# A decoder layer on one core: the opening stage computes its modulation sums, its normalised rows and its angles another way

## The chip, the cores and the metric

The kernel runs on one core of a Trainium2 chip. A core has five engines that run their own instruction streams: TensorE (PE in the profile, with PEld for its weight loads), VectorE (DVE), ScalarE (ACT), GpSimd (POOL) and SyncE (SP, which here only issues transfers). The metric is the device time of one execution in microseconds (us); lower is better.

## The reference, cut to what matters

The layer maps x (1024 rows of 1024 channels, float32) to an output of the same shape. A vector c gives six modulation vectors; the first two, shift sh1 and scale sc1, are used in the opening:

```python
cond = silu(c)
mod = einsum('bd,de->be', cond, w_ada) + b_ada     # 1024 x 6144 weights
sh1, sc1, gt1, sh2, sc2, gt2 = split(mod, 6)
h = rmsnorm(x, g_mix) * (1 + sc1) + sh1
proj = h @ w_in                                    # q, k, v, indexer q, indexer k, weights, conv
```

Then q, k and the indexer's q and k are rotated by angles `position * inv_freq`, top-k sparse attention and a causal convolution run side by side, `w_out` joins them, and an MLP of width 4096 and a final norm follow. Every product that the kernel takes for h is made of three products of two-part operands (a rounded part "hi" and the remainder "lo").

## The kernel before, in words

Everything is one Python function, `layer`, which writes instructions for all engines; a planner then lays out, ahead of the run, the order of each engine's instructions, by the number in `tc.cur_priority` and by its own estimate of when operands are ready. Each engine then runs its list strictly in that order. In the opening the number simply follows the order in which the lines are written; afterwards the table `PR` gives it by kind of work. Waits between engines are made from the data that instructions read and write, and a tile with `bufs=n` makes the next writer wait until the oldest of n copies is no longer read.

The opening stage lies in the pool `start`. Its loads are issued on SP in the order of the string `START`: x0 to x7 are the eight 128-row blocks of x (`xs`, 512 KB each), a0 to a3 are quarters of the first two modulation vectors' weights (`wa`, each quarter two tiles of 1 MB, one for contraction blocks 0 to 3, one for 4 to 7; four tiles in all, so that quarter 2 takes the space of quarter 0 and quarter 3 that of quarter 1), p0 to p2 are the pieces of `w_in` for k, v, the indexer's k and weights. Its work is written in the order of `WORK`:

- `row_scale(g)` takes the mean square of four blocks of rows, two by ACT (`Square`, L290) and two by DVE (L287), and makes for each block a diagonal matrix `dg` of 1/rms (L296); it is called for blocks 0 to 3 first and as step r4 for blocks 4 to 7.
- step t (`transposes`) multiplies the eight 128 x 128 parts of a block by `dg` on TensorE, which transposes and scales them (L309); ACT copies the result to `xT` (L310). t0 to t3 are the first half of the rows, t4 to t7 the second.
- step a (`ada`) sums, on DVE, a quarter's eight weight blocks times `cond` into `acc` (L318, seven times L316). Step e (`ada_end`) sums `acc` over partitions by four one-column matmuls into `pa` (L324) and finishes scale and shift in `modT` (L326 to L329). A quarter serves two of the eight channel blocks.
- step h (`h_cols`) makes two channel blocks of h for the first half of the rows: DVE scales in place in `xT` (L334), ACT writes the hi part (L335), DVE (channel blocks 0 to 5) or POOL (6 and 7) the lo part (L336). For the second half of the rows the same runs after all steps, with POOL for every lo part.
- step k (`kv`) adds two channel blocks to the k/v products of blocks 0 to 3 (L347), in four PSUM tiles (`mm`, `mc`).

After the steps the angles are computed from `positions` (L374 to L412): eight small products, a range reduction of some twenty dependent small DVE instructions, and three ACT instructions. When the pool is closed, the k/v products of blocks 0 to 3 are evacuated (L447 to L450: ACT and DVE), and the same four PSUM tiles take blocks 4 to 7 ("the second k/v round", again L347, 96 matmuls). Then come the projections for the indexer's q (L137), keys are rotated and stacked (L457 to L482), and the other four modulation vectors are summed on DVE from 512 KB loads (`ada_part`, loads L517, sums L521 and L523; `ada_row` L530, `ada_col` L537).

Of the kernel before, what the change touches and what calls it, by code (L numbers as in the profile page):

```python
# [9 lines left out]
FT = mybir.dt.float32  # L10
# [17 lines left out]
EPS = 1e-6  # L28
# [44 lines left out]
def layer(ctx, tc, x, c, positions, w_ada, b_ada, g_mix, w_in, conv_w, conv_b,  # L73
          conv_norm_g, conv_norm_b, w_out, g_mlp, w_up, w_down, g_final, out, dump=None):
    nc = tc.nc
    V, A, P, T, SP = nc.vector, nc.scalar, nc.gpsimd, nc.tensor, nc.sync
    x, positions = x[0], positions[0]
# [10 lines left out]
    def dbg(name, ap):  # L88
        if dump and name in dump:
            SP.dma_start(dump[name], ap)  # L90
# [134 lines left out]
    pieces = []  # L225
# [6 lines left out]
    def hblk(b, k, s):  # L232
        return hT[b // 4][s][:, k, (b % 4) * 128:(b % 4 + 1) * 128]
# [4 lines left out]
    hT = {}  # L238
    with tc.tile_pool(name="start", bufs=1, reuse_waits="tile") as st:
# [39 lines left out]
        ms, rs, tmp1 = (st.tile([128, 8], FT, name=n) for n in ("ms", "rs", "tmp1"))  # L279
        junk = st.tile([128, D], U8, name="junk")  # L280
        dg = {}

        def row_scale(g0):
            for b in range(g0, g0 + 4):
# [6 lines left out]
            col = slice(g0, g0 + 4)  # L291
            V.tensor_scalar(ms[:, col], ms[:, col], 1.0 / D, EPS, op0=OP.mult, op1=OP.add)
            rsqrt(rs[:, col], ms[:, col], tmp1[:, col], 4)
            for b in range(g0, g0 + 4):
                dg[b] = st.tile([128, 128], FT, name="dg", bufs=4)
                V.tensor_scalar(dg[b], ident, rs[:, b:b + 1], None, op0=OP.mult)  # L296

        for hf in range(2):  # L300
            hT[hf] = (half_tile("AC"[hf]), half_tile("BD"[hf]))
        pa = psum.tile([128, 16], FT, name="po")

        def transposes(b):
            for q in range(2):
                t = tp_tile()
                for j in range(4):
                    k = 4 * q + j
                    T.matmul(t[:, j, :], xs[b][:, k * 128:(k + 1) * 128], dg[b], start=True, stop=True)  # L309
                A.copy(xT[:, 4 * q:4 * q + 4, b * 128:(b + 1) * 128], t)  # L310

        def ada(jj):
# [6 lines left out]
            return acc  # L319

        def ada_end(jj, acc):
            for i in range(4):
                c0 = 8 * (i // 2) + 2 * jj + i % 2
                T.matmul(pa[:, c0:c0 + 1], acc[:, i * 128:(i + 1) * 128], ones[:, 0:1], start=True, stop=True)  # L324
            s0, s1 = slice(2 * jj, 2 * jj + 2), slice(8 + 2 * jj, 10 + 2 * jj)
            V.tensor_tensor(modT[:, s0], pa[:, s0], bada[:, s0], op=OP.add)  # L326
            a1 = modT[:, s1]
            V.tensor_tensor(a1, pa[:, s1], bada[:, s1], op=OP.add)
            V.scalar_tensor_tensor(a1, a1, 1.0, gmix[:, s0], op0=OP.add, op1=OP.mult)  # L329

        def h_cols(k, hf):
            hi, lo = hT[hf]
            xk = xT[:, k, hf * 512:(hf + 1) * 512]
            V.tensor_scalar(xk, xk, modT[:, 8 + k:9 + k], modT[:, k:k + 1], op0=OP.mult, op1=OP.add)  # L334
# [3 lines left out]
        kvps = {}  # L338

        def kv(k, blocks):  # L340
            for i, b in enumerate(blocks):
                if k == 0:
                    kvps[b] = (mm_tile if i < 2 else mc_tile)(328)
                hi, lo = hblk(b, k, 0), hblk(b, k, 1)
                wh, wl = pieces[k]
                for j, (l, r) in enumerate(((hi, wh), (lo, wh), (hi, wl))):
                    T.matmul(kvps[b], l, r, start=k == 0 and j == 0, stop=k == KD - 1 and j == 2)  # L347

        row_scale(0)
        accs = {}  # L350
        for step in WORK.split():
            n = int(step[1:])
            if step[0] == "a":
                accs[n] = ada(n)
            elif step[0] == "t":
                transposes(n)
            elif step[0] == "r":
                row_scale(n)
            elif step[0] == "e":
                ada_end(n, accs[n])  # L360
            elif step[0] == "h":
                for k in (2 * n, 2 * n + 1):
                    h_cols(k, 0)
            elif step[0] == "k":
                for k in (2 * n, 2 * n + 1):
                    kv(k, KVG[0])
            elif step[0] == "g":
                for k in (2 * n, 2 * n + 1):
                    h_cols(k, 1)
        for k in range(KD):  # L370
            if k // 2 not in [int(x[1:]) for x in WORK.split() if x[0] == "g"]:
                h_cols(k, 1)
        posf = st.tile([8, 128], FT, name="posf")
        V.tensor_copy(posf, posi)  # L374
        tq = tp_tile()
# [35 lines left out]
        V.tensor_scalar(ml, ml, -1.0, 1.5707963267948966, op0=OP.mult, op1=OP.add)  # L411
        A.activation(cs, ml, AF.Sin)  # L412

        tw = tp_tile()
# [4 lines left out]
        for k in range(KD):  # L419
            dbg("hT", xT[:, k, :]) if k == 0 else None  # L420
# [844 lines left out]
```

## Time and profile before

| | us |
|---|---|
| median of 3 runs | 1375.25 (1374.19 to 1385.54) |
| the profiled execution, whole | 1377.54 |
| its span, first to last instruction | 1375.8 |
| mean granted TensorE clock | 0.964 of full |
| PE busy | 1268.3 |
| DVE busy | 974.8 |
| ACT busy | 683.5 |
| POOL busy | 482.0 |

Times in the rows are microseconds from the span's start. A chain of waits names, step by step, what the last instruction was waiting for; a table of stretches gives each engine's busy time and the clock within it; a wait row names the instruction that waited, the one that released it, the total, the number of times and the longest.

### The profile page before, as it was taken

The page shows a single profiled execution, that of the slowest core. Times are in us where ns is not written, and L with a number is a line of the kernel's source. Part 1 is how long each engine was busy: PE and PEld are TensorE (multiplying, and loading weights), DVE is VectorE, ACT ScalarE, POOL GpSimd, SP SyncE. Part 2 cuts the span into 40 slices and gives each one's busy share as a digit, 9 for nine tenths or more (in the row PEclk, how much of TensorE's full clock was granted, in tenths as well). Part 3 has the DMA queues.
Part 4 walks back from the last instruction along what each step waited for, and adds up shares of the span by engine and source line. Part 5 has one row for each costly group of instructions (what it writes and reads, how often), then busy time and mean ns, then how long its engine had stood idle before and what let it go on. Part 6 is the DMA issues. An engine that isn't in the chain of part 4 may idle for free.

```text
span 1375.8 us, 19421 instructions
## 1 busy us (share of the span) xinstructions
PE 1268.3 (92%) x6686; PEld 1065.7 (77%) x6686; DVE 974.8 (71%) x2074; ACT 683.5 (50%) x1376; POOL 482.0 (35%) x396
## 2 busy tenths in 40 slices
PE   4677899989998899989999999899999999999997
PEld 4676789978887678767887879777878877888875
DVE  4879889999898899997878762473443386343457
ACT  3323358855764888768983552333122223333332
POOL 1333434422144234452223216422222244444453
PEclk9688999999999899999999999999999999999999
DMA  9337735522143123222111122352111134323332
GB/s 319 121 115 224 226 79 155 139 62 70 31 139 110 60 70 93 92 70 61 62 47 54 62 77 85 130 192 83 47 45 49 54 107 162 93 91 101 94 98 91
DMA packets 135690, 139.55 MB, mean 101 GB/s; under 512 B 8877, under 2 KB 109833, under 8 KB 135592
## 3 DMA queue, kind: packets, MB, share of 16 engines
q1 hardware_dynamic: 135424, 138.22, 32.2%
q8 instruction: 52, 0.85, 0.3%
q14 instruction: 46, 0.38, 0.1%
q10 hardware_dynamic: 168, 0.11, 0.0%
HBM read 126.23 MB, written 12.06 MB: 101 GB/s over the span
## 4 chain that ended last, share of the span: by engine, by line
PE 68%; DVE 21%; DMA 4%; issue 3%; ACT 3%; POOL 1%; ACTq 0%; POOLq 0%; DVEq 0%; SPq 0%
PE mm L126 25%; PE mc L126 13%; PE mm L137 9%; PE tp L126 7%; DMA wa<-in_w_ada_dram 3%; PE po L841 2%; PE tp L834 2%; DVE acc L521 2%; DVE cv L643 1%; PE tp L309 1%; PE po L748 1%; PE mc L592 1%; DVE acc L1018 1%; PE mc L822 1%; DVE acc L316 1%
## 5 line engine op out<-in xcount | busy, mean ns | idle before, releaser
L185 POOL TENSOR_TENSOR wlo<-wraw,whi 128x512 fp32r<-128x512 f32 x310 | 416.7, 1352 | 754.2 <-ACT whi L184 698.0
L184 ACT ACTIVATE whi<-wraw 128x512 fp32r<-128x512 f32 x310 | 193.9, 629 | 292.1 <-PE mm L126 143.1
L126 PE MATMUL mm<-half,whi 128*128 128x512 f32 x608 | 207.4, 407 | 0.6 <-ACT half L957 0.6
L680 ACT ACTIVATE sj<-score,bits 128x512 uint8<-128x512 f32 (+5 forms) x186 | 163.2, 877 | 23.0 <-DVE bits L683 11.0
L643 DVE SCALAR_TENSOR_TENSOR cv<-glu,cwT,cv 128x512 f32<-128x512 f32 x232 | 174.0, 750 | 0.8
L126 PE MATMUL mm<-whi,uh 128*128 128x512 f32 x344 | 141.7, 412 | 14.3 <-DVE sq L979 8.2
L126 PE MATMUL mc<-half,whi 128*128 128x512 f32 x416 | 149.0, 390 | 0.1
L126 PE MATMUL mm<-whi,ul 128*128 128x512 f32 x344 | 138.8, 404 | 3.0 <-DVE ul L986 3.0
L126 PE MATMUL mm<-wlo,uh 128*128 128x512 f32 x344 | 139.4, 405 | 0.0
L984 DVE TENSOR_TENSOR sq<-sq 128x512 f32<-128x512 f32 x42 | 46.0, 1096 | 126.1 <-ACT sq L983 126.1
L1018 DVE TENSOR_TENSOR acc<-mm,acc 128x512 f32<-128x512 f32 x152 | 104.3, 687 | 39.8 <-PE mm L126 38.9
L126 PE MATMUL mc<-half,wlo 128*128 128x512 f32 x336 | 131.1, 390 | 0.0
L126 PEld LDWEIGHTS mm<-half,whi 128*128 128x128 f32 x608 | 114.2, 192 | 20.0 <-ACT half L957 0.8
L137 PE MATMUL mm<-whi,half 128*128 128x256 f32 x640 | 121.8, 286 | 3.2 <-DVE wi L450 3.0
L126 PE MATMUL mm<-half,wlo 128*128 128x512 f32 x304 | 123.1, 405 | 0.0
L137 PEld LDWEIGHTS mm<-whi,half 128*128 128x128 f32 x640 | 102.9, 194 | 5.7 <-issue 3.1
L126 PE MATMUL mc<-h,whi 128*128 128x512 f32 x256 | 99.9, 390 | 0.0
L126 PEld LDWEIGHTS mm<-whi,uh 128*128 128x128 f32 x344 | 66.5, 193 | 37.0 <-DVE sq L979 10.8
L137 PE MATMUL mm<-wlo,half 128*128 128x256 f32 x320 | 91.2, 285 | 0.0
L126 PEld LDWEIGHTS mc<-half,whi 128*128 128x128 f32 x416 | 78.0, 188 | 16.6 <-ACT half L957 0.5
L126 PEld LDWEIGHTS mm<-whi,ul 128*128 128x128 f32 x344 | 66.6, 194 | 18.7 <-DVE ul L986 4.3
L126 PEld LDWEIGHTS mm<-wlo,uh 128*128 128x128 f32 x344 | 66.8, 194 | 13.2
(312 smaller groups left out, 2657.4 us busy)
## 6 DMA issues: line engine op xcount, KB each, us to landing
wraw<-in_w_up_dram SPq DMA_DIRECT2D x108, 256.0 KB, 2.8
wraw<-in_w_down_dram SPq DMA_DIRECT2D x108, 256.0 KB, 2.8
wa<-in_w_ada_dram SPq DMA_DIRECT2D x48, 512.0 KB, 4.5
wraw<-in_w_in_dram SPq DMA_DIRECT2D x33, 256.0 KB, 2.8
wraw<-in_w_in_dram SPq DMA_DIRECT2D x64, 128.0 KB, 2.9
wraw<-in_w_out_dram SPq DMA_DIRECT2D x32, 256.0 KB, 2.7
xs<-in_x_dram SPq DMA_DIRECT2D x8, 512.0 KB, 4.5
x<-in_x_dram SPq DMA_DIRECT2D x8, 512.0 KB, 4.3
```

The lines of the kernel that those rows point to most:

```text
L126: T.matmul(ps, x, y, start=first and i == 0, stop=last and i == 3 * n - 1)
L137: T.matmul(ps[:, i * 256:(i + 1) * 256], rows[i][k][x], w[k][y], start=m == 0, stop=m == len(steps) - 1)
L184: A.activation(hi, raw, AF.Copy)
L185: P.tensor_tensor(lo, raw, hi.bitcast(FT), op=OP.subtract)
L309: T.matmul(t[:, j, :], xs[b][:, k * 128:(k + 1) * 128], dg[b], start=True, stop=True)
L521: V.scalar_tensor_tensor(accs[s], w, cond[:, k:k + 1], accs[s], op0=OP.mult, op1=OP.add)
L643: V.scalar_tensor_tensor(y if tap == CK - 1 else s, gl[:, tap:tap + 512], cwT[:, j, tap:tap + 1], s, op0=OP.mult, op1=OP.add)
L680: A.activation(sj[:, :L], score[b], AF.Sign, bias=bits[:, col].bitcast(FT), accum_out=cnt[:, col])
L834: T.transpose(t[:, 2 * i + u, :], sbp[u][:, (i0 + i) * 128:(i0 + i + 1) * 128], ident)
L841: T.matmul(po[:, hp % 2], vhl[:, i0 + i, g].rearrange("p a d -> p (a d)"), p[:, 2 * i:2 * i + 2, :], start=i0 + i + j == 0, stop=i0 + i == ...
L984: V.tensor_tensor(sq, sq, sq, op=OP.mult)
L1018: V.tensor_tensor(acc[b][:, cols], ps, acc[b][:, cols], op=OP.add)
```

## The change

The orders become

```diff
-START = "x0 x1 x2 x3 a0 p0 x4 x5 x6 x7 a1 p1 a2 p2 a3"
-WORK = "a0 t0 t1 t2 t3 e0 h0 a1 e1 k0 h1 a2 e2 k1 r4 t4 t5 h2 a3 e3 k2 h3 k3 t6 t7"
+START = "x0 x1 x2 x3 a0 p0 a1 p1 x4 x5 a2 p2 x6 x7 a3"
+WORK = "a0 t0 t1 t2 t3 e0 h0 a1 e1 k0 h1 a2 e2 k1 h2 a3 e3 k2 h3 k3 r4 g0 g1 g2 g3"
-LOV = 6
```

The block that computes the angles is written, unchanged, ahead of `row_scale(0)` instead of behind the last step. `xT` keeps only the first half of the rows. The functions change thus:

```diff
-        xT = st.tile([128, KD, S], FT, name="xT")
+        xT = st.tile([128, KD, 512], FT, name="xT")
...
         def row_scale(g0):
             for b in range(g0, g0 + 4):
-                if b % 2:
-                    xv = xs[b].rearrange("p (u n) -> p u n", u=2)
-                    V.tensor_tensor_reduce(xT[:, b - b % 2:b - b % 2 + 2, 512:], xv, xv, 1.0, 0.0, op0=OP.mult, op1=OP.add,
-                                           accum_out=ms[:, b:b + 1])
-                else:
-                    A.activation(junk, xs[b], AF.Square, accum_out=ms[:, b:b + 1])
+                A.activation(junk, xs[b], AF.Square, accum_out=ms[:, b:b + 1])
...
         def ada(jj):
-            acc = st.tile([128, 512], FT, name="acc", bufs=2)
-            for k in range(KD):
-                if k:
-                    V.scalar_tensor_tensor(acc, was[jj, k // 4 * 4][:, k % 4, :], cond[:, k:k + 1], acc, op0=OP.mult, op1=OP.add)
-                else:
-                    V.tensor_scalar(acc, was[jj, k // 4 * 4][:, k % 4, :], cond[:, 0:1], None, op0=OP.mult)
+            ps = cv_tile()
+            for k in range(4):
+                T.matmul(ps[0:1, :], cond[:, k:k + 1], was[jj, 0][:, k, :], start=k == 0, stop=k == 3)
+            rowp[jj] = st.tile([1, 512], FT, name="rowp", bufs=2)
+            A.copy(rowp[jj], ps[0:1, :])
+            acc = st.tile([128, 512], FT, name="acc", bufs=2)
+            V.tensor_scalar(acc, was[jj, 4][:, 0, :], cond[:, 4:5], None, op0=OP.mult)
+            for k in range(5, KD):
+                V.scalar_tensor_tensor(acc, was[jj, 4][:, k % 4, :], cond[:, k:k + 1], acc, op0=OP.mult, op1=OP.add)
             return acc
 
         def ada_end(jj, acc):
             for i in range(4):
                 c0 = 8 * (i // 2) + 2 * jj + i % 2
-                T.matmul(pa[:, c0:c0 + 1], acc[:, i * 128:(i + 1) * 128], ones[:, 0:1], start=True, stop=True)
+                T.matmul(pa[:, c0:c0 + 1], rowp[jj][:, i * 128:(i + 1) * 128], ones[0:1, 0:1], start=True, stop=False)
+                T.matmul(pa[:, c0:c0 + 1], acc[:, i * 128:(i + 1) * 128], ones[:, 0:1], start=False, stop=True)
...
         def h_cols(k, hf):
             hi, lo = hT[hf]
-            xk = xT[:, k, hf * 512:(hf + 1) * 512]
+            if hf == 0:
+                xk = xT[:, k, :]
+            else:
+                t = tp_tile()
+                for b in range(4):
+                    T.matmul(t[:, b, :], xs[4 + b][:, k * 128:(k + 1) * 128], dg[4 + b], start=True, stop=True)
+                xk = t.rearrange("p a b -> p (a b)")
+            A.activation(hi[:, k, :], xk, AF.Identity, bias=modT[:, k:k + 1], scale=modT[:, 8 + k:9 + k])
             V.tensor_scalar(xk, xk, modT[:, 8 + k:9 + k], modT[:, k:k + 1], op0=OP.mult, op1=OP.add)
-            A.activation(hi[:, k, :], xk, AF.Copy)
-            (V if hf == 0 and k < LOV else P).tensor_tensor(lo[:, k, :], xk, hi[:, k, :].bitcast(FT), op=OP.subtract)
+            V.tensor_tensor(lo[:, k, :], xk, hi[:, k, :].bitcast(FT), op=OP.subtract)
```

So a quarter's contraction blocks 0 to 3 are summed on TensorE into one row, which ACT copies to `rowp`; blocks 4 to 7 stay on DVE; `ada_end` adds both into `pa`. The second half of the rows is transposed channel block by channel block in the new steps g0 to g3 (two blocks each), its h is made in PSUM without a copy to `xT`, and POOL takes no lo part of h any more. All mean squares are ACT's.

## Rows read from the trace of the kernel before

**Rows 1.** The page, busy time and share of the span of each engine.
```profile
PE 1268.3 (92%) x6686; PEld 1065.7 (77%) x6686; DVE 974.8 (71%) x2074; ACT 683.5 (50%) x1376; POOL 482.0 (35%) x396
```

**Rows 2.** Table of stretches: PE, PEld, DVE, ACT, POOL busy; clock; transfer share; GB/s.
```profile
0.00:104.00 104.00, 65.21 (x360) 62.38 (x361) 70.95 (x157) 32.97 (x63) 29.53 (x29) 0.82 0.57 186
104.00:200.00 96.00, 82.87 (x421) 68.26 (x420) 82.97 (x179) 39.52 (x81) 35.81 (x34) 0.89 0.62 182
...
16.00:32.00 16.00, 12.46 (x76) 12.11 (x76) 10.77 (x23) 8.45 (x14) 2.26 (x1) 0.93 1.07 360
48.00:64.00 16.00, 9.07 (x32) 8.24 (x32) 14.44 (x25) 3.30 (x6) 7.76 (x5) 0.61 0.23 73
```

**Rows 3.** Timeline of PE, the opening: start, duration, instruction, idle before and releaser.
```profile
16.89 10.35 PE L309 MATMUL tp<-dg,xs 128*128 128x128 f32 x64 [8.64 <-DVE dg L296]
27.08 0.95 PE L324 MATMUL po<-ones,acc 128*128 128x1 f32 x8
...
37.27 7.23 PE L309 MATMUL tp<-dg,xs 128*128 128x128 f32 x62
44.34 0.95 PE L324 MATMUL po<-ones,acc 128*128 128x1 f32 x8
...
73.78 1.60 PE L324 MATMUL po<-ones,acc 128*128 128x1 f32 x8 [1.64 <-DVE acc L316]
...
82.54 0.31 PE L347 MATMUL mc<-wlo,half 128*128 128x328 f32 x1
87.99 0.89 PE L347 MATMUL mm<-whi,half 128*128 128x328 f32 x2 [5.13 <-DVE wi L450]
...
103.74 0.31 PE L347 MATMUL mc<-wlo,half 128*128 128x328 f32 x1
```

**Rows 4.** Groups of DVE instructions by shape, 0 to 104 us: busy, mean ns, idle before.
```profile
L316 DVE SCALAR_TENSOR_TENSOR acc<-wa,cond,acc 128x512 f32<-128x512 f32 x28 | 23.8, 849 | 0.5
L334 DVE TENSOR_SCALAR xT<-xT,modT 128x512 f32<-128x512 f32 x16 | 11.0, 725 | 0.1
L287 DVE CUSTOM_DVE_ANT_0 xT<-xs 128x1024 f32<-128x1024 f32 x4 | 4.9, 1223 | 8.4 <-DMA xs<-in_x_dram 8.4
```

**Rows 5.** Timeline of POOL, then of DVE and ACT, in the opening's end.
```profile
77.17 5.21 POOL L336 TENSOR_TENSOR half<-xT,half 128x512 fp32r<-128x512 f32 x4 [4.00 <-ACT half L335]
...
78.68 1.27 DVE L393 TENSOR_SCALAR mh<-mh 128x64 f32<-128x64 f32 x1
...
86.44 0.26 ACT L412 ACTIVATE cs<-ml 128x64 f32<-128x64 f32 x1 [0.26 <-DVE ml L411]
```

**Rows 6.** Tile wa, 0 to 62 us (min/median/max in ns, of landing in us); SP's waits.
```profile
L318 DVE TENSOR_SCALAR acc<-wa,cond x4: 476/482/1495, 17.3 to 61.4; 128x512 f32<-128x512 f32 x4
DMA to landing us min/median/max: 3.5/8.9/10.0
...
SPq L255 <- DVE acc L316: 7.2, 2, 5.4
```

**Rows 7.** Timeline of PE: a float32 matmul of 512 columns at either clock.
```profile
1014.01 1.02 PE L530 MATMUL po<-g2acc,ones 128*128 128x512 f32 x2
...
129.14 2.08 PE L530 MATMUL po<-acc,ones 128*128 128x512 f32 x2 [6.20 <-DVE gt L531]
```

**Rows 8.** Lines L958, L959 and L290: duration ns min/median/max, first and last start.
```profile
L958 DVE TENSOR_SCALAR tp<-tp,modT x16: 810/818/819, 453.5 to 902.6; 128x512 f32<-128x512 f32 x16
...
L959 DVE TENSOR_TENSOR half<-tp,half x8: 680/682/693, 454.9 to 470.4; 128x512 fp32r<-128x512 f32 x8
...
L290 ACT ACTIVATE junk<-xs x4: 1041/1056/1078, 6.9 to 31.1; 128x1024 uint8<-128x1024 f32 x4
```

**Rows 9.** Evacuation after the first k/v round: first ACT copy, last DVE piece.
```profile
86.60 0.25 ACT L447 COPY kk<-mm 128x128 f32<-128x128 f32 x1
...
88.05 0.17 DVE L450 TENSOR_SCALAR wi<-mc 128x8 f32<-128x8 f32 x1
```

**Rows 10.** SP's first load of the later modulation parts; waits for space and of PE.
```profile
82.41 0.82 SPq L517 DMA_DIRECT2D wa<-in_w_ada_dram  x2
...
SPq L517 <- POOL half L336: 22.3, 1, 22.3
...
PE po L530 <- DVE gt L531: 6.2, 1, 6.2
```

More of the change, by code (lines that the diff above doesn't have):

```diff
@@ L300, in layer @@
[L300 to L312, printed above, removed]
-            acc = st.tile([128, 512], FT, name="acc", bufs=2)
-            for k in range(KD):
-                if k:
-                    V.scalar_tensor_tensor(acc, was[jj, k // 4 * 4][:, k % 4, :], cond[:, k:k + 1], acc, op0=OP.mult, op1=OP.add)
-                else:
-                    V.tensor_scalar(acc, was[jj, k // 4 * 4][:, k % 4, :], cond[:, 0:1], None, op0=OP.mult)
-            return acc
@@ L321, in ada_end @@
-        def ada_end(jj, acc):
-            for i in range(4):
-                c0 = 8 * (i // 2) + 2 * jj + i % 2
-                T.matmul(pa[:, c0:c0 + 1], acc[:, i * 128:(i + 1) * 128], ones[:, 0:1], start=True, stop=True)
[L325 to L329, printed above, removed]
@@ L331, in h_cols @@
-        def h_cols(k, hf):
-            hi, lo = hT[hf]
-            xk = xT[:, k, hf * 512:(hf + 1) * 512]
-            V.tensor_scalar(xk, xk, modT[:, 8 + k:9 + k], modT[:, k:k + 1], op0=OP.mult, op1=OP.add)
-            A.activation(hi[:, k, :], xk, AF.Copy)
-            (V if hf == 0 and k < LOV else P).tensor_tensor(lo[:, k, :], xk, hi[:, k, :].bitcast(FT), op=OP.subtract)
[L338 to L369, printed above, removed]
@@ L370, in layer @@
-        for k in range(KD):
-            if k // 2 not in [int(x[1:]) for x in WORK.split() if x[0] == "g"]:
-                h_cols(k, 1)
         posf = st.tile([8, 128], FT, name="posf")
@@ L412, in layer, with row_scale @@
         A.activation(cs, ml, AF.Sin)
+        xT = st.tile([128, KD, 512], FT, name="xT")
+        ms, rs, tmp1 = (st.tile([128, 8], FT, name=n) for n in ("ms", "rs", "tmp1"))
+        junk = st.tile([128, D], U8, name="junk")
+        dg = {}
+        def row_scale(g0):
+            for b in range(g0, g0 + 4):
+                A.activation(junk, xs[b], AF.Square, accum_out=ms[:, b:b + 1])
+            col = slice(g0, g0 + 4)
+            V.tensor_scalar(ms[:, col], ms[:, col], 1.0 / D, EPS, op0=OP.mult, op1=OP.add)
+            rsqrt(rs[:, col], ms[:, col], tmp1[:, col], 4)
+            for b in range(g0, g0 + 4):
+                dg[b] = st.tile([128, 128], FT, name="dg", bufs=4)
+                V.tensor_scalar(dg[b], ident, rs[:, b:b + 1], None, op0=OP.mult)
@@ new lines, in layer, with transposes @@
+        for hf in range(2):
+            hT[hf] = (half_tile("AC"[hf]), half_tile("BD"[hf]))
+        pa = psum.tile([128, 16], FT, name="po")
+        def transposes(b):
+            for q in range(2):
+                t = tp_tile()
+                for j in range(4):
+                    k = 4 * q + j
+                    T.matmul(t[:, j, :], xs[b][:, k * 128:(k + 1) * 128], dg[b], start=True, stop=True)
+                A.copy(xT[:, 4 * q:4 * q + 4, b * 128:(b + 1) * 128], t)
+        rowp = {}
@@ new lines, in ada @@
+        def ada(jj):
+            ps = cv_tile()
[7 more added lines that the diff above has]
+                V.scalar_tensor_tensor(acc, was[jj, 4][:, k % 4, :], cond[:, k:k + 1], acc, op0=OP.mult, op1=OP.add)
+            return acc
@@ new lines, in ada_end @@
+        def ada_end(jj, acc):
+            for i in range(4):
+                c0 = 8 * (i // 2) + 2 * jj + i % 2
+                T.matmul(pa[:, c0:c0 + 1], rowp[jj][:, i * 128:(i + 1) * 128], ones[0:1, 0:1], start=True, stop=False)
+                T.matmul(pa[:, c0:c0 + 1], acc[:, i * 128:(i + 1) * 128], ones[:, 0:1], start=False, stop=True)
+            s0, s1 = slice(2 * jj, 2 * jj + 2), slice(8 + 2 * jj, 10 + 2 * jj)
+            V.tensor_tensor(modT[:, s0], pa[:, s0], bada[:, s0], op=OP.add)
+            a1 = modT[:, s1]
+            V.tensor_tensor(a1, pa[:, s1], bada[:, s1], op=OP.add)
+            V.scalar_tensor_tensor(a1, a1, 1.0, gmix[:, s0], op0=OP.add, op1=OP.mult)
@@ new lines, in h_cols @@
+        def h_cols(k, hf):
+            hi, lo = hT[hf]
+            if hf == 0:
+                xk = xT[:, k, :]
+            else:
+                t = tp_tile()
+                for b in range(4):
+                    T.matmul(t[:, b, :], xs[4 + b][:, k * 128:(k + 1) * 128], dg[4 + b], start=True, stop=True)
+                xk = t.rearrange("p a b -> p (a b)")
+            A.activation(hi[:, k, :], xk, AF.Identity, bias=modT[:, k:k + 1], scale=modT[:, 8 + k:9 + k])
+            V.tensor_scalar(xk, xk, modT[:, 8 + k:9 + k], modT[:, k:k + 1], op0=OP.mult, op1=OP.add)
+            V.tensor_tensor(lo[:, k, :], xk, hi[:, k, :].bitcast(FT), op=OP.subtract)
@@ new lines, in layer, with kv @@
+        kvps = {}
+        def kv(k, blocks):
+            for i, b in enumerate(blocks):
+                if k == 0:
+                    kvps[b] = (mm_tile if i < 2 else mc_tile)(328)
+                hi, lo = hblk(b, k, 0), hblk(b, k, 1)
+                wh, wl = pieces[k]
+                for j, (l, r) in enumerate(((hi, wh), (lo, wh), (hi, wl))):
+                    T.matmul(kvps[b], l, r, start=k == 0 and j == 0, stop=k == KD - 1 and j == 2)
+        row_scale(0)
+        accs = {}
+        for step in WORK.split():
+            n = int(step[1:])
+            if step[0] == "a":
+                accs[n] = ada(n)
+            elif step[0] == "t":
+                transposes(n)
+            elif step[0] == "r":
+                row_scale(n)
+            elif step[0] == "e":
+                ada_end(n, accs[n])
+            elif step[0] == "h":
+                for k in (2 * n, 2 * n + 1):
+                    h_cols(k, 0)
+            elif step[0] == "k":
+                for k in (2 * n, 2 * n + 1):
+                    kv(k, KVG[0])
+            elif step[0] == "g":
+                for k in (2 * n, 2 * n + 1):
+                    h_cols(k, 1)
@@ L417, in layer @@
         V.tensor_scalar(cwT, tw[:, :, :CK], 0.5, None, op0=OP.mult)
-        for k in range(KD):
-            dbg("hT", xT[:, k, :]) if k == 0 else None
     att = ctx.enter_context(ExitStack())
```

11 lines of the change are left out of this document (removed).

## The prediction, made before the changed kernel was run

> **What bounds the kernel now.** I read first the page's busy times: TensorE works 1268.3 of 1375.8 us, so the whole kernel is near TensorE's own work [rows 1]. Next the table of stretches, to see where TensorE is not busy: of the 107.5 us that it idles, 104.00 − 65.21 = 38.8 lie in the first 104 us, and another 13.1 in the next 96 [rows 2]. There its clock is low too: 0.61 of full from 48 to 64 us, that is mostly 1.2 GHz instead of 2.4, against 0.93 from 16 to 32 [rows 2]. So the opening can be shortened, and what follows it is TensorE's stream, which moves forward with it.
>
> Then TensorE's timeline, for the opening's milestones [rows 3]. The first transposes start at 16.89; the four quarters' one-column sums start at 27.08, 44.34, about 61.5 (not shown) and 73.78; the first k/v round ends at 82.85, the second starts at 87.99 and ends at 104.05. Between the first sum and the second lie 7.23 us of transposes of the second half. From 44 to 82 us TensorE mostly waits, and the groups of DVE say for what [rows 4]: DVE has 70.95 us of work in these 104, hardly idle behind 17 us. Its sums L316 cost 23.8, the scaling L334 11.0. Both means are above what one of them needs undisturbed: L318, a two-operand scaling of the same size, has a median of 0.482 and a maximum of 1.495 [rows 6], and the long ones stand beside POOL's lo parts such as the four that take 5.21 from 77.17 [rows 5]. The transfers are no bound there: 360 GB/s from 16 to 32 us but 73 from 48 to 64 [rows 2]. DVE is late; the angles at the end are the same engine's work, from 78.68 until the cosine at 86.44 [rows 5], and the evacuation waits behind that cosine in ACT's list: 86.60 [rows 9].
>
> **The change part by part.**
>
> First quarter. Squares: ACT's takes 1.06, DVE's took 1.22 [rows 8, 4]; block 3 lands last either way, so nothing. The row sum adds four float32 matmuls of 512 columns, 1.02 each at the full clock and 2.08 at the low one, two trace records a matmul [rows 7]: 4.1 or 8.3 us on TensorE, ahead of or among the transposes; eight small ones more in step e, 0.95 for eight [rows 3]. DVE's half (0.48 + 3 x 0.85 = 3.0 [rows 6, 4]) is hidden by the transposes. If the sum fits in the 8.64 us idle before the transposes it costs nothing. I take +4: step e at 32 instead of 28; bounds 0 and +9. The one-partition copy on ACT lies between zero and a full copy, and is in the +4.
>
> Second to fourth quarters. Gone from DVE: 16 of 28 sums (16 x 0.85 = 13.6 us), two of four L287 squares' worth in mid-chain (2.4), and the lengthening beside POOL of L334 (11.0 − 16 x 0.5 = 3.0); gone from TensorE's way are the 7.23 us of transposes. Then DVE is not late any more, and next late are the loads. A quarter has 2 MB, x 4 MB, the k/v pieces 1.3 MB: 13.9 million bytes in all, at 360 GB/s 39 us; with the slow first 4 us, at the earliest about 43. Quarters 2 and 3 need the tiles of 0 and 1 free, which SP waited 7.2 us for already [rows 6]. Quarter 0's tiles are free when its row sum is done, at about 31; quarter 1's at about 36. Quarter 3 then stands in SP's list behind x6, x7, and takes 8.9 us to land (10.0 at most) [rows 6]: about 46. Its row sum is 4.1, step e with modT 2: the fourth quarter is finished at 52, where before it was at 75.4. I take 23 us gained; bounds 18 (landing at 50) and 28 (loads never paused).
>
> Steps h3 and k3 keep their 7.4 us: two scalings fewer, but two lo parts now on DVE instead of POOL.
>
> Angles. They move into DVE's idle time before block 3 lands, 8.4 us in the row of L287 [rows 4], and beside the transposes; ACT's three small instructions fit there. Without that gap they would cost their 7.8 us again. At the end they free the evacuation: from the last k/v matmul to the second round there are 5.14 us [rows 3]; evacuation itself needs 88.05 − 86.60 + 0.17 = 1.6 [rows 9]. Gain 3.4; none, if its space is still held by the second half's x.
>
> Second half. The 64 transposing records and their 7.23 us are moved, not removed, and fall between the second round's matmuls unless they fit in a wait. Each channel block needs DVE twice, 0.82 + 0.68 = 1.5 us [rows 8], 12 us for eight, on a DVE that is otherwise free by then; the second round takes 2 us a block, so DVE stays ahead. Step r4 (four squares of 1.06 [rows 8] and a few small instructions) runs on ACT, POOL and DVE while the last quarter loads. I take half the transposes as uncovered: +3; bounds 0 and +8.
>
> Sum: −23 − 3.4 + 3, so the second round ends at about 80 instead of 104.
>
> Behind it. The later modulation parts' first loads wait for space in the opening's pool: now 22.3 us, until POOL's last lo part, issued at 82.41, 22 us before the second round's end [rows 10]. Then the last reader is the last step g, at about 66, 14 us before that end. So this chain moves only 16 us forward, TensorE's stream 24; and in its in-order list stand L530 and L537, with the projections queued behind them, where it already waited 6.2 us [rows 10]. I take 2 us given back; bounds 0 and 10. The planner also lays out the rest anew; TensorE idles 107.5 − 38.8 = 68.7 us there, and I allow a tenth of it, 7 us, either way.
>
> Net −22. The profiled execution took 1377.54, which is 1375.8 span and 1.7 around it; this is 2.3 above the median. 1377.5 − 22 = 1355.5, less 2.3: **1353 us**.
>
> One rule speaks against the row sums. The page "TensorE: Matmul & The Clock Gate" of the Trainium skill, section "HAM oscillation — how this bites in real kernels", says that bursts of matmuls parted by waits for data each begin at the lower clock, so that restructuring around such waits pays at every burst. The trace agrees where waits part the bursts, with its 0.61 [rows 2]. At the low clock the sum comes to 1365 (first rival), at the full one to 1353. I take the full one: the new order has transposes and k/v steps to fill the gaps between row sums, as from 16 to 32 us now.
>
> **The rivals.**
>
> *Low clock (12%).* TensorE idles before each quarter and runs its sum at 1.2 GHz: 2.08 instead of 1.02 for each of 16 matmuls, 17 us, of which about 12 stand in the chain. For it: the clock of 48 to 64; against: 0.93 from 16 to 32 [rows 2]. 1353 + 12 = 1365. The page named above gives the rule for it.
>
> *Loads (12%).* SP is in order, so quarter 2 waiting for its tiles holds back x6, x7 and quarter 3, and a row sum placed late in TensorE's list frees them late. Each microsecond costs one. Landing at 56 instead of 46 gives 1363. For it: the wait of 7.2 and the 73 GB/s; against: DVE's half is short.
>
> *Larger gain (8%).* The first row sum hides in the idle 8.64, loads never pause, the transposes hide in waits, nothing is given back: 28 + 3.4 = 31.4 gives 1344, and 1337 with the planner's 7 us on this side. For it: the transfers' 360 GB/s held for 16 us; against: only four weight tiles.
>
> *No doing (4%).* The planner orders by its own estimate and could leave the angles late or put the second half's blocks ahead of the last k/v steps; then only the sums' 13.6 us help, less the row sums' 4 and 4 for DVE's added lo parts: about 1370.
>
> *Slower (6%).* One mechanism: the later modulation parts. TensorE's list has their matmuls at planned places; if the loads wait not for step g but for a tile read later, say by the evacuated keys, TensorE stops at L530 and L537 for three parts. The gain before it is 24, so it decides from a stall of 24 on, and slower by over 1% needs 38, that is 13 a part, twice the 6.2 seen. 1392.
>
> **How the numbers follow.** The forecast has 58%. A measurement here tells about 1% (14 us, below 1361.5) from no change. Most of the forecast's own range, 1345 to 1362, is faster (0.55), the larger gain too (0.08); low clock and loads lie near the bound, about a third faster (0.08): 0.71. The same: the rest of these two (0.16), 0.03 of the forecast and 0.03 of the fourth rival: 0.22. Slower: 0.07. The range 1337 to 1368 leaves out the slower case, the fourth rival and the outer parts of the low-clock and load cases, about 0.18.
>
> **What will show it.** After the change: angles done before 17 us and no wait of the evacuation for the cosine; DVE in the first 80 us well below 70 and L334 back at 0.5; step e of the fourth quarter at 50 to 55, TensorE's wait before its row sum being on the load; second round's end at 78 to 84, its matmuls with transposes between; from there to the end the same distance as now, 1272 us, give or take 8. Wrong would be: a fourth quarter later than 60, row-sum matmuls at 2 us, a second round that starts over 4 us behind the first, or a distance behind the round that grows by over 10.

## The result: 0.6% slower where a gain was forecast

Sixteen runs of the changed kernel have a median of 1383.89 us (1376.64 to 1391.21), sixteen of the kernel before 1374.81; the ratio is 1.0058, with an interval of 1.0036 to 1.0080. Forecast were 1353, in a range of 1337 to 1368. By the prediction's own bound of about 1% this is no change, but the interval excludes any gain. The profiled execution took 1385.62 with a span of 1383.8; that span is 8.0 longer than before's 1375.8.

First the page of the changed kernel, its engines' busy times, which answer to [rows 1]:

```profile
PE 1291.2 (93%) x6750; PEld 1073.4 (78%) x6750; DVE 955.9 (69%) x2060; ACT 688.7 (50%) x1380; POOL 467.8 (34%) x386
```

TensorE has 22.9 us more to do, DVE 18.9 less: the work went where the change sent it. Next the table of stretches of the changed kernel, with the columns of [rows 2]; the first one is the whole opening, up to the end of the second k/v round:

```profile
0.00:109.20 109.20, 85.31 (x425) 67.67 (x426) 53.76 (x143) 37.96 (x67) 15.15 (x19) 0.86 0.54 177
16.00:32.00 16.00, 15.49 (x72) 10.26 (x73) 6.94 (x30) 4.87 (x10) 2.26 (x1) 0.89 1.03 338
32.00:48.00 16.00, 14.86 (x68) 11.23 (x67) 9.13 (x15) 8.38 (x13) 2.28 (x1) 0.80 0.90 300
48.00:64.00 16.00, 15.21 (x67) 10.36 (x66) 6.57 (x19) 4.82 (x8) 2.62 (x2) 0.88 0.11 33
64.00:80.00 16.00, 15.41 (x76) 12.66 (x75) 9.67 (x19) 4.32 (x6) 0.00 (x0) 0.79 0.00 1
```

Before, TensorE was busy for 9.07 of the 16 us from 48 on and DVE for 14.44; now it is 15.21 and 6.57, and the transfers are over by then (33 GB/s, later 1). The opening has changed from one that waits for DVE into one that waits for TensorE, and it ends at 109.0 instead of 103.9. TensorE's timeline of the changed kernel says how, with the columns of [rows 3]:

```profile
16.51 5.90 PE L354 MATMUL cv<-wa,cond 128*1 128x512 f32 x8 [8.87 <-DMA wa<-in_w_ada_dram]
22.34 2.99 PE L344 MATMUL tp<-dg,xs 128*128 128x128 f32 x24
25.27 0.38 PE L366 MATMUL po<-ones,rowp 1*128 1x1 f32 x2
25.57 0.38 PE L367 MATMUL po<-ones,acc 128*128 128x1 f32 x2
...
27.68 6.38 PE L344 MATMUL tp<-dg,xs 128*128 128x128 f32 x40
33.99 3.59 PE L354 MATMUL cv<-wa,cond 128*1 128x512 f32 x8
...
38.46 0.38 PE L366 MATMUL po<-ones,rowp 1*128 1x1 f32 x2
38.77 0.42 PE L396 MATMUL mm<-wlo,half 128*128 128x328 f32 x1
...
40.92 0.38 PE L367 MATMUL po<-ones,acc 128*128 128x1 f32 x2 [1.14 <-DVE acc L360]
...
43.50 0.59 PE L367 MATMUL po<-ones,acc 128*128 128x1 f32 x2
...
49.03 3.59 PE L354 MATMUL cv<-wa,cond 128*1 128x512 f32 x8
...
63.16 3.59 PE L354 MATMUL cv<-wa,cond 128*1 128x512 f32 x8
...
67.62 0.38 PE L366 MATMUL po<-ones,rowp 1*128 1x1 f32 x2
...
69.60 0.28 PE L367 MATMUL po<-ones,acc 128*128 128x1 f32 x2
...
71.36 0.38 PE L367 MATMUL po<-ones,acc 128*128 128x1 f32 x2
...
80.32 0.31 PE L396 MATMUL mc<-wlo,half 128*128 128x328 f32 x1
80.47 1.95 PE L381 MATMUL tp<-dg,xs 128*128 128x128 f32 x16
84.06 1.13 PE L381 MATMUL tp<-dg,xs 128*128 128x128 f32 x8 [1.65 <-DVE half L385]
...
87.73 2.05 PE L381 MATMUL tp<-dg,xs 128*128 128x128 f32 x8 [0.65 <-DVE half L385]
...
93.15 0.64 PE L396 MATMUL mc<-whi,half 128*128 128x328 f32 x1 [2.81 <-DVE wi L453]
...
109.01 0.45 PE L484 MATMUL tp<-identr,nh 128*128 128x128 f32 x4
```

The last row, the keys' transposes, marks the second round's end in all kernels below. The reader is to see four things:

- The list has hardly a gap from 16.5 to 80.6: 1.14 us at 40.92, and 0.79 and 0.59 in places not shown.
- Step e is no longer one run of eight records but sixteen, in pairs of L366 (from the copied row) and L367 (from `acc`), and in the second to fourth quarters other matmuls stand behind the first L366. The fourth quarter's is done at 71.7, against 75.4 before.
- Between the first round's end at 80.6 and the second's start at 93.15 lie 12.5 us, where before there were 5.1 [rows 3].
- The clock falls with each step e. In a table of stretches of 1 us the grant is 0.50 or 0.51, that is 1.2 GHz, from 28 to 31, from 42 to 48, from 59 to 62 and from 73 to 79 us, and mostly 1.00 between. The runs of step e's one-column matmuls ahead of these falls last from 25.3 to 27.8, 40.9 to 44.1, 55.5 to 57.7 and 69.6 to 71.7 us. Ahead of the first fall TensorE had no wait, ahead of the others one of 1.14, 0.79 and 0.59 us. What runs at half clock then are transposes and k/v matmuls.

DVE's groups by shape of the changed kernel, 0 to 109 us, for [rows 4], and after them its largest wait:

```profile
L360 DVE SCALAR_TENSOR_TENSOR acc<-wa,cond,acc 128x512 f32<-128x512 f32 x12 | 11.0, 920 | 0.3
...
L384 DVE TENSOR_SCALAR tp<-tp,modT 128x512 f32<-128x512 f32 x8 | 6.5, 816 | 6.0 <-ACT half L383 6.0
...
L384 DVE TENSOR_SCALAR xT<-xT,modT 128x512 f32<-128x512 f32 x8 | 4.3, 543 | 7.7 <-ACT half L383 7.7
```

```profile
DVE modT L369 <- PE po L367: 20.0, 4, 7.1
```

The sums fell from 23.8 to 11.0 us, and the scaling in place runs at 543 ns a piece instead of 725. But DVE now waits for step e, 20.0 us in four times.

### The profile page after: what moved, and what is told of

Read it like the earlier page. It is cut to its first block, busy times and chain, and to the rows that moved or that the text cites. A ratio compares the mean times of both kernels' runs of the same rounds, so it can differ in the third digit from the quotient of the medians.

```text
span 1383.8 us, 19533 instructions
## 1 busy us (share of the span) xinstructions
PE 1291.2 (93%) x6750; PEld 1073.4 (78%) x6750; DVE 955.9 (69%) x2060; ACT 688.7 (50%) x1380; POOL 467.8 (34%) x386
## 4 chain that ended last, share of the span: by engine, by line
PE 72%; DVE 18%; DMA 4%; ACT 2%; issue 2%; POOL 1%; ACTq 0%; SPq 0%; POOLq 0%; DVEq 0%
PE mm L125 24%; PE mc L125 14%; PE mm L136 9%; PE tp L125 7%; DMA wa<-in_w_ada_dram 4%; PE po L844 2%; PE tp L837 2%; DVE acc L524 2%; DVE cv L646 1%; PE po L751 1%; DVE acc L1021 1%; DVE e L661 1%; PE mc L825 1%; PE mc L595 1%; PE cv L354 1%
## 5 line engine op out<-in xcount | busy, mean ns | idle before, releaser
L125 PEld LDWEIGHTS mm<-whi,uh 128*128 128x128 f32 x344 | 66.1, 192 | 36.1 <-DVE acc L1021 9.8
```

Of the source, the lines that this page charges most:

```text
L125: T.matmul(ps, x, y, start=first and i == 0, stop=last and i == 3 * n - 1)
```

## The experiments

Times are medians; the ratio is against runs of the kernel before on the same chip, with its 95% interval. "e3" is the end of the fourth quarter's step e and "end" the second k/v round's end, both from the one profiled run of each kernel. The runs of the kernel before beside them had medians of 1372.38 to 1375.32, so differences between two rows of medians are uncertain by some us.

| kernel | median | ratio | e3 | end |
|---|---|---|---|---|
| before | 1374.81 | 1 | 75.4 | 103.9 |
| after | 1383.89 | 1.0058 [1.0036, 1.0080] | 71.7 | 109.0 |
| x1_dve_sums | 1369.99 | 0.9954 [0.9932, 0.9976] | 63.7 | 100.0 |
| x3_angles_late | 1388.87 | 1.0096 [1.0063, 1.0129] | 74.0 | 115.4 |
| x4_g_early | 1379.30 | 1.0036 [1.0012, 1.0060] | 75.6 | 103.1 |
| y1_angles | 1373.59 | 0.9983 [0.9967, 1.0000] | 73.0 | 95.8 |
| y3_load_order | 1382.43 | 1.0054 [1.0029, 1.0079] | 68.0 | 108.0 |
| v3_angles_loads | 1376.68 | 1.0018 [0.9994, 1.0041] | 66.5 | 96.9 |
| w1_fold | 1371.16 | 0.9966 [0.9934, 0.9997] | 63.4 | 97.6 |
| z1_dve_g_early | 1366.50 | 0.9938 [0.9907, 0.9969] | 69.5 | 95.0 |
| z2_dve_ahead | 1367.65 | 0.9958 [0.9924, 0.9992] | 66.5 | 96.0 |
| v1_fold_g_early | 1364.21 | 0.9917 [0.9883, 0.9951] | 68.5 | 95.8 |
| v2_fold_ahead | 1368.66 | 0.9957 [0.9936, 0.9979] | 66.1 | 95.9 |

**Is it the sums on TensorE?** `x1_dve_sums` is the changed kernel with every sum on DVE again and step e from `acc` alone:

```diff
-            ps = cv_tile()
-            for k in range(4):
-                T.matmul(ps[0:1, :], cond[:, k:k + 1], was[jj, 0][:, k, :], start=k == 0, stop=k == 3)
-            rowp[jj] = st.tile([1, 512], FT, name="rowp", bufs=2)
-            A.copy(rowp[jj], ps[0:1, :])
...
-                T.matmul(pa[:, c0:c0 + 1], rowp[jj][:, i * 128:(i + 1) * 128], ones[0:1, 0:1], start=True, stop=False)
-                T.matmul(pa[:, c0:c0 + 1], acc[:, i * 128:(i + 1) * 128], ones[:, 0:1], start=False, stop=True)
+                T.matmul(pa[:, c0:c0 + 1], acc[:, i * 128:(i + 1) * 128], ones[:, 0:1], start=True, stop=True)
```

> The changed kernel with the first two modulation vectors summed wholly on DVE again (the row sums and their one-row matmuls are gone from TensorE); all else as changed. Theory P, TensorE became the opening's bound (15.2 to 15.5 of every 16 us from 16 to 80 us): the fourth quarter's scale and shift are done at 56 us, give or take 4, instead of 72; the first k/v round ends near 66 instead of 80; the second round ends near 96 instead of 109; the kernel takes 1371 us. Theory L, the loads are late: the fourth quarter not before 68, kernel unchanged at 1384. Theory D, DVE becomes late again: the fourth quarter at 70 to 75, kernel 1384.

It gave 1369.99, 13.9 below the changed kernel and just faster than before. So the part of the change that was to bring most cost more than the rest brought. Its table of stretches, the opening:

```profile
0.00:100.00 100.00, 65.37 (x359) 61.85 (x360) 64.58 (x159) 35.30 (x63) 15.67 (x19) 0.85 0.59 193
```

TensorE has its 65.4 us of before, not 85.3; the fourth quarter is finished at 63.7 although DVE again makes all 28 sums. That is later than the 56 expected, and DVE is the late engine in it again, as in TensorE's timeline of x1, where step e of the fourth quarter waits for `acc` (that of the third waited 3.48):

```profile
62.70 1.05 PE L363 MATMUL po<-ones,acc 128*128 128x1 f32 x8 [2.15 <-DVE acc L355]
```

**The row sums, or how they are joined?** `w1_fold` keeps the sixteen row-sum matmuls on TensorE, but joins them to the rest on DVE: one addition on one partition, so that neither ACT's copy nor the one-row matmuls of step e are needed.

```diff
-            rowp[jj] = st.tile([1, 512], FT, name="rowp", bufs=2)
-            A.copy(rowp[jj], ps[0:1, :])
...
+            V.tensor_tensor(acc[0:1, :], acc[0:1, :], ps[0:1, :], op=OP.add)
...
-                T.matmul(pa[:, c0:c0 + 1], rowp[jj][:, i * 128:(i + 1) * 128], ones[0:1, 0:1], start=True, stop=False)
-                T.matmul(pa[:, c0:c0 + 1], acc[:, i * 128:(i + 1) * 128], ones[:, 0:1], start=False, stop=True)
+                T.matmul(pa[:, c0:c0 + 1], acc[:, i * 128:(i + 1) * 128], ones[:, 0:1], start=True, stop=True)
```

> The changed kernel with the row sum of TensorE added to row 0 of acc by one DVE instruction, so that the copy to rowp and the one-row matmuls in step e (8 records a quarter, with the others 2.5 to 3.3 us instead of 0.95 to 1.6) are gone; the row sums stay. Theory P: each quarter 1.5 us earlier, the second round ends at 103 to 105 instead of 109, kernel 1379 us; with x1 (9 us earlier) that splits TensorE's added work into row sums and pairs. Theory that only the row sums' place in TensorE's list counts: no change, 1384 us.

It gave 1371.16, 12.7 below the changed kernel and level with x1: far more than the 5 us expected. TensorE's timeline of w1, and its table of stretches:

```profile
29.95 0.95 PE L365 MATMUL po<-ones,acc 128*128 128x1 f32 x8
30.83 3.59 PE L354 MATMUL cv<-wa,cond 128*1 128x512 f32 x8
...
38.80 1.05 PE L365 MATMUL po<-ones,acc 128*128 128x1 f32 x8 [1.62 <-DVE acc L359]
...
50.25 0.95 PE L365 MATMUL po<-ones,acc 128*128 128x1 f32 x8
...
62.47 0.95 PE L365 MATMUL po<-ones,acc 128*128 128x1 f32 x8
...
97.58 0.46 PE L482 MATMUL tp<-identr,nh 128*128 128x128 f32 x4
```

```profile
16.00:32.00 16.00, 15.54 (x83) 9.41 (x84) 7.58 (x29) 6.33 (x13) 2.28 (x1) 1.00 1.07 348
32.00:48.00 16.00, 14.17 (x55) 7.28 (x54) 13.52 (x20) 7.55 (x12) 4.95 (x2) 0.89 0.99 324
48.00:64.00 16.00, 13.62 (x81) 10.04 (x79) 9.51 (x26) 4.12 (x6) 1.02 (x1) 1.00 0.01 2
```

Step e is one run of 0.95 to 1.05 us again, and the quarters are done at 30.9, 39.9, 51.2 and 63.4, against 27.8, 44.1, 57.7 and 71.7 in the changed kernel. So what the change lost is the joining: ACT's copy, one-row matmuls, and the places that the planner gives them among the k/v matmuls, together 8.3 us at the fourth quarter and 11.4 at the second round's end. The two timelines, counted from each start to the next up to the end of the fourth step e, say where the 8.3 lie: the four steps e take 3.7 us instead of 10.5, and the first half's transposes and the three steps k, the same records in both, 20.3 instead of 25.3; waits, row sums and step g take 3.8 more, and the first row sum starts 0.3 earlier. The 5.0 of the transposes and steps k go with the clock: in w1 the grant is 0.50 only from 42 to 44 us in this stretch. That the one-column pairs are what lowers it was not varied alone. The row sums themselves neither cost nor bring: 1371.2 with them, 1370.0 without, with intervals that overlap.

**The second half's h behind everything.** `x4_g_early` is the changed kernel with steps r4 and g written between the others. `v1_fold_g_early` does it to w1, `z1_dve_g_early` to x1.

```diff
-WORK = "a0 t0 t1 t2 t3 e0 h0 a1 e1 k0 h1 a2 e2 k1 h2 a3 e3 k2 h3 k3 r4 g0 g1 g2 g3"
+WORK = "a0 t0 t1 t2 t3 e0 h0 a1 e1 k0 r4 g0 h1 a2 e2 k1 g1 h2 a3 e3 k2 g2 h3 k3 g3"
```

> The changed kernel with r4 and the steps g0 to g3 written between the steps of the first half instead of behind k3. Theory E, the stretch between the two k/v rounds is empty because the second half's h is made there and nothing of the next pool is laid out before it is done: the second round starts at most 6 us behind the first round's end instead of 12.7, and ends at 103 to 105 instead of 109; the kernel takes 1379 us. Theory P alone, TensorE's work in the opening is the sum that counts: the transposes only move ahead, the second round still ends at 108 to 109, kernel 1384.

> Sums wholly on DVE as in x1_dve_sums, and the second half's steps written between the first half's as in x4_g_early. If what x1 left is theory E's stretch between the two k/v rounds (13 us there), the second round ends at 93 to 95 instead of 100.0, and the kernel takes 1364 us. If DVE, busy 12 to 14 of each 16 us again, has no room for the second half's h before the first round is done, the round ends at 99 to 101 and the kernel takes 1370 us.

> w1_fold (row sums on TensorE, added to acc by DVE, no one-row matmuls) with the second half's steps written early as in z1_dve_g_early. If the two gains add (w1 ended the second round at 97.6 with 13 us between the rounds; z1 took 5 us off x1), the round ends at 91 to 93 and the kernel takes 1363 to 1366 us, below z1's 1366.5. If TensorE, busy 13.6 to 15.5 of each 16 us from 16 to 64 us in w1, has no room for the transposes, the round ends at 97 and the kernel takes 1371 us.

All three have a lower median than their partner: by 4.6 us (x4), 3.5 (z1) and 7.0 (v1), though the intervals of each pair overlap. v1, at 1364.21, has the lowest median of the study (z1's interval overlaps with its own): by its ratio 0.83% below the kernel before, by the medians 19.7 us below the changed one. ScalarE's timeline says what the gap was. In the changed kernel:

```profile
89.82 0.78 ACT L383 ACTIVATE half<-tp,modT 128x512 fp32r<-128x512 f32 x1 [1.92 <-PE tp L381]
90.50 0.26 ACT L450 COPY kk<-mm 128x128 f32<-128x128 f32 x1
```

and in v1:

```profile
76.53 0.78 ACT L381 ACTIVATE half<-tp,modT 128x512 fp32r<-128x512 f32 x1 [4.11 <-PE tp L379]
77.21 0.26 ACT L448 COPY kk<-mm 128x128 f32<-128x128 f32 x1
```

In both the first evacuating copy stands right behind the last hi part of the opening, however long the products have been ready: since 80.6 in the changed kernel, since 76.3 in v1. What the g steps make behind k3 delays the evacuation: 9.9 us there, 0.9 in v1. In v1 there are 3.5 us between the rounds instead of 12.5, TensorE's timeline:

```profile
75.97 0.31 PE L394 MATMUL mc<-wlo,half 128*128 128x328 f32 x1
76.11 0.38 PE L379 MATMUL tp<-dg,xs 128*128 128x128 f32 x2
76.43 0.43 PE L419 MATMUL tp<-identr,cwr 31*128 31x31 f32 x4
79.76 0.53 PE L394 MATMUL mm<-whi,half 128*128 128x328 f32 x2 [2.91 <-DVE wi L451]
```

x4 mends this loss alone: with the pairs still there its fourth quarter is even later (75.6), and the second round starts at 88.7.

The early g steps have a price: the fourth quarter comes 3.8 us later in x4 than in its partner, 5.8 in z1 and 5.1 in v1. The gap between the rounds shrinks from 12.5 to 4.2 us, from 9.3 to 1.7 and from 10.3 to 3.5 (not from 13, which two of the expectations took), but the second round's end gains only 5.9, 5.0 and 1.8. v1's time was as expected, its end, 95.8 instead of 91 to 93, was not: of the 7.3 us between w1's span and v1's (1369.7 and 1362.4) 5.5 lie behind the second round and are not explained.

**More order.** `z2_dve_ahead` and `v2_fold_ahead` write each quarter's sums one quarter ahead, against z1 and v1:

```diff
-WORK = "a0 t0 t1 t2 t3 e0 h0 a1 e1 k0 r4 g0 h1 a2 e2 k1 g1 h2 a3 e3 k2 g2 h3 k3 g3"
+WORK = "a0 t0 t1 t2 t3 a1 e0 h0 k0 a2 e1 h1 k1 r4 a3 e2 g0 h2 k2 g1 e3 h3 k3 g2 g3"
```

> As z1_dve_g_early, but each quarter's sum is written ahead of the step e and h of the quarter before it (a1 before e0, a2 before e1, a3 before e2), so that DVE sums while the other engines finish a quarter. If the quarters in x1 (12.4 us apart) are held by DVE's order, not by its load, they come closer: fourth quarter at 57 instead of 64, second round's end at 88 to 91, kernel 1360 us. If the loads of quarters 2 and 3 or DVE's load hold them, the end is that of z1, 94 to 100, kernel 1364 to 1370 us.

> As v1_fold_g_early with each quarter's sum written ahead of the step e before it, as in z2_dve_ahead. Expected the same as v1, 91 to 94 and 1363 to 1366 us, since z2 gave nothing over z1. If the quarters' distance in w1 (12 us) comes from the order of the sums and not from loads, 88 and 1360 us.

The fourth quarter comes 2.4 to 3.0 us earlier, the second round's end does not (96.0 and 95.9, against 95.0 and 95.8), and the times are 1.2 and 4.5 us longer than their partners', with intervals that overlap. This order brought nothing; v2's 4.5 us lie behind the opening and are not explained.

**Angles, and the order of the loads.** `x3_angles_late` is the changed kernel with the angles' block moved back behind the last step. `y1_angles` is the kernel before with that block moved to the start, `y3_load_order` the kernel before with the new order of loads, `v3_angles_loads` both.

```diff
-START = "x0 x1 x2 x3 a0 p0 x4 x5 x6 x7 a1 p1 a2 p2 a3"
+START = "x0 x1 x2 x3 a0 p0 a1 p1 x4 x5 a2 p2 x6 x7 a3"
```

> The changed kernel with the angles computed behind the last step again. By the prediction's step the evacuation waits for the cosine again and the second k/v round starts 3.4 us later: kernel 1387 us. Rival: DVE has free time from 20 to 80 us in the changed kernel, the planner lays the angles there, and nothing moves: 1384 us.

> The kernel before with one part of the change alone: the angles computed ahead of row_scale(0). By the prediction's step the second k/v round starts 3.4 us earlier (84.5 instead of 88.0), kernel 1371 us. If DVE sets the opening's end of the kernel before, some 11 us of small instructions leave its late stretch and the round starts at 79 to 80: kernel 1366 us. Rival: the last lo parts on POOL hold the pool as long as before (82.4), start at 84.5 or later, kernel 1371 to 1375 us.

> The kernel before with one part of the change alone: quarters 1 and 2 loaded ahead of the second half's x. In the kernel before DVE never waits for a quarter, so nothing is gained; step r4, which is written ahead of k2, waits for x7 behind the tiles of quarter 0, so DVE may stand still for it. Expected 1375 us, second round's end 104; up to 5 us later if r4 waits.

> The kernel before with two parts of the change: the angles early and quarters 1 and 2 loaded first. Alone they ended the second round at 95.8 and at 108.0 (before: 103.9). If the load order is bad in itself (r4 late, DVE late), both together end at about 100, kernel 1378 us. If its 7 us were only the angles, left behind the last step together with the second half's scaling, the first round's earlier end (74.5 instead of 82.9) comes through: the second round ends at 92 to 94, kernel 1366 us.

Late angles make the changed kernel's median 5.0 us longer (the intervals overlap; the two profiled spans differ by 0.8). x3's timeline of DVE and then of TensorE shows the chain: the angles' last operation, and the second round behind it, 5.7 us later than in the changed kernel.

```profile
97.14 0.20 DVE L415 TENSOR_SCALAR ml<-ml 128x64 f32<-128x64 f32 x1 [0.47 <-ACT ml L414]
```

```profile
98.82 0.92 PE L354 MATMUL mm<-whi,half 128*128 128x328 f32 x2 [8.65 <-DVE wi L453]
```

In the kernel before, early angles bring the second round's end from 103.9 to 95.8, but the time only by 1.2 to 2.3 us (0.17% by the ratio). The new order of loads alone makes it 0.54% slower. The table of stretches of y3, and TensorE's wait in it, say why: the fourth quarter is done at 68.0 instead of 75.4, but the second half's rows now come last, and their scaling and the angles stand in DVE's list behind the first half's work, up to 90 us, with the evacuation behind them.

```profile
80.00:96.00 16.00, 4.51 (x16) 4.54 (x17) 14.34 (x50) 3.20 (x14) 4.83 (x4) 0.50 0.34 108
```

```profile
91.49 0.89 PE L347 MATMUL mm<-whi,half 128*128 128x328 f32 x2 [15.09 <-DVE wi L450]
```

With the angles early as well (v3) the second round's end is 96.9, no better than y1's 95.8, and its time, 1376.7, is near the 1378 expected if the order of the loads is bad in itself. From v3 to x1, that is with the rebuilt h, the new order of work and the squares dealt out anew, the ratio falls by 0.64 points; so this group paid. Its members were not run apart, and it did not pay in the opening: x1's second round ends later than v3's (100.0, not 96.9), so the gain lies behind it and is not explained. The ladder of ratios: angles 0.9983, loads too 1.0018, h and order too 0.9954, half of the sums on TensorE 1.0058, these joined by DVE 0.9966, g steps early 0.9917.

## Why the prediction was wrong, step by step

**The step that failed: "Then DVE is not late any more, and next late are the loads ... the fourth quarter is finished at 52."** Next late was TensorE itself. The fourth quarter's weights, the last in the order `START`, were through by 47 us, near the forecast 46: the transfers run at 238 GB/s from 46 to 47 us and at 3 from 47 to 48. The fourth row sum began only at 63.16, when TensorE's list had come to it. The prediction checked DVE and the transfers, and never added up what TensorE has to do from the first transposes to that point; it read TensorE as mostly waiting from 44 to 82 us, where its own row has it busy for 9.07 of 16, at 0.61 [rows 2]. Its own terms do it: the first half's transposes 10.35 [rows 3], four row sums of 4.1, three steps k at a quarter of the second round's 16.06 [rows 3], 12.0, and four steps e of 0.95 + 0.95 [rows 3], 7.6: 46.4 us, so from 16.5 at the earliest 62.9. Only 35.5 us lie between 16.5 and 52. The third step k is written behind the fourth step e in `WORK`, and the planner put it ahead; without it the sum ends at 58.9, still too late. w1, with row sums and without pairs, comes at 63.4; TensorE is busy there for 15.5, 14.2 and 13.6 of the 16 us from 16, 32 and 48. (x1's 63.7 is no measure of this sum: it has no row sums, and waits for DVE.)

In the changed kernel it took 55.2 us, from 16.51 to 71.7. By its timeline, from each start to the next: row sums 16.4, transposes of the first half 9.2, steps e 10.5, ten records of step g's transposes 1.1, waits 1.9, the three steps k 16.0, in part at half clock. Against the 46.4 that is 2.9 more for step e, 4.0 for the steps k, 3.0 for step g and waits, 1.1 less for the transposes. So the price of step e was mis-sized (10.5 us for four, where the prediction's rows give 7.6), and the half clock behind it was not in the sum at all. ACT's copy and the places of the pairs in the list were not run apart from the pairs.

**"I take half the transposes as uncovered: +3"** failed too. Second half and evacuation together were to leave 1.7 us between the rounds and 3 within the second; there were 12.5 between and, at 15.9 for the round, nothing within. The transposes did not fall between the second round's matmuls: three of the eight channel blocks (24 of 64 records) ran from 68.48 on, ahead of and within k3, the other five stood behind k3, one after another with waits for DVE (1.65 us at 84.06), and the evacuation behind all of them. The prediction had named the risk for the angles ("none, if its space is still held by the second half's x") and not carried it over to the g steps, which are the opening's last instructions as the angles were. x4, z1 and v1 agree: with these steps earlier the gap is 4.2, 1.7 and 3.5 us.

Together: the second round's end was forecast at 80.1 (52 + 7.4 + 1.7 + 16 + 3) and came at 109.0. Of the 28.9 the fourth quarter has 19.7, h3 and k3 1.5 (8.9 instead of 7.4), the gap with the round 7.7. A small slip beside it: −23 − 3.4 + 3 is −23.4, which the prediction carried on as 24 and as a net −22; the sum gives 1354, not 1353.

**What held.** The row sums took 3.59 us for a quarter, 5.90 for the first, where 4.1 was taken and 8.3 was the bound. The low clock did not come as the first rival had it, on the row sums: from 48 to 64 us the grant rose from 0.61 [rows 2] to 0.88, with TensorE busy for 15.21 of the 16 us instead of 9.07. It came behind the steps e, on transposes and steps k, which no part of the prediction priced. The rule of the Trainium skill that the prediction set against the row sums ("TensorE: Matmul & The Clock Gate", section "HAM oscillation — how this bites in real kernels") speaks of bursts parted by waits; the trace agrees where the waits went, from 48 to 64 us, and the fall at 28 us, with TensorE busy for every us from 24 on, is another case. The first quarter was done at 27.8, where 32 was taken. DVE's work in the opening fell to 53.8 us. The loads were no rival: 33 GB/s from 48 us on. Of the signs of being wrong that the prediction named, two came (a fourth quarter later than 60, a second round over 4 us behind the first); a third, row-sum matmuls at 2 us, only in the first row sum, whose longest record, two of which make a matmul, took 1.06 us.

The angles' last DVE instruction ended at 20.1 us and the cosine at 20.4, not before 17; TensorE was in the first row sum until 22.4, so nothing there waited for them. Two rows of DVE's timeline show the first of the diagonals, which were made between the range reduction's instructions, and the reduction's last instruction 3.1 us later:

```profile
16.83 0.28 DVE L331 TENSOR_SCALAR dg<-identr,rs 128x128 f32<-128x128 f32 x1
...
19.94 0.20 DVE L314 TENSOR_SCALAR ml<-ml 128x64 f32<-128x64 f32 x1 [0.47 <-ACT ml L313]
```

Their gain, 3.4 by the prediction, is 5.7 at the second round's start and 5.0 between the medians by x3.

**Behind the opening** the distance from the second round's end to the end of the span grew from 1271.9 to 1274.8 (1383.8 − 109.0), within the 8 allowed; of the 8.0 us that the span grew, 5.1 lie in the opening. The slower rival, the later modulation parts, would have needed 13 us for each of three; it did not occur: TensorE's one wait for `gt` there is 6.4 us, where it was 6.2 [rows 10]. This distance is 1266 to 1278 over all thirteen kernels, without a pattern by the length of the opening, and as one profiled run each gives it; the sixteen runs of the kernel before alone lie 18 us apart. So the end of the second round alone does not give the time. y1's is 1276.0, so that half of the 8.1 us it gained went again. In y1 the attention of the second half's rows starts its last product 20 us earlier than before (795.9, not 816.0), but the norm ahead of the MLP its last transpose only 4.8 (895.5, not 900.3). What takes the rest in that stretch stays open.

## What to carry to other kernels

When work is taken from a late engine, add up the whole list of the engine that receives it, from the first free moment to the milestone that is promised, before naming the next bound; here that was one sum of four rows, and it forbade the forecast. Moving half of a sum to TensorE is worth no more than its joining is cheap: one 0.67 us addition on DVE did in w1 and v1 what took a copy and four one-row matmuls a quarter, and the half clock behind them, in the changed kernel. Steps that are written last in a stage held back the evacuation that the planner laid out behind it; written between the others they cost 4 to 6 us at the fourth quarter instead, and gained 2 to 6 at the second round's end.

## What the runs showed of the hardware

A float32 matmul from one partition, one column wide, is no cheaper than one from 128: in the changed kernel's first step e, at a grant of 1.00, a matmul (two records) lasts 0.38 us and the next begins after 0.31, for L366 with one row as for L367 with 128. That is 0.155 a record; in one run, before, eight took 0.95, 0.12 each. The grant fell to half behind four such steps e, the first time from 28 us on without a wait of TensorE before it.

A DVE sum beside POOL's lo part of the weights is longer: this one took 2.79 us, where the others of L360 take about 0.75, in the changed kernel's timelines of DVE and of POOL (in w1 one of 2.80 stands beside a POOL piece of 3.18). So the prediction's undisturbed 0.482 of L318 is no measure for a sum: that is 0.75.

```profile
36.81 2.79 DVE L360 SCALAR_TENSOR_TENSOR acc<-wa,cond,acc 128x512 f32<-128x512 f32 x1
```

```profile
36.77 2.28 POOL L143 TENSOR_TENSOR wlo<-wraw,whi 128x984 fp32r<-128x984 f32 x1 [9.39 <-DMA wraw<-in_w_in_dram]
```

In the changed kernel the first row sum, behind 8.87 us of waiting, took 5.90 us, each later one, in an unbroken stream, 3.59.
